# Six gate columns of a hybrid decoder layer as three Strassen pairs, behind an S5 branch with a shorter rhythm

## The chip, the cores and the metric

The kernel runs on one core of a Trainium2 chip. Its time is the device time of one launch in microseconds (us). An engine's name is short: PE is TensorE (matmul), DVE is VectorE, ACT is ScalarE, POOL is GpSimd, SP is the sync engine, which here issues nearly all DMA transfers.

## What is computed

One decoder layer on 1024 tokens of width 1024, in float32. All of the input projection's columns are products of the same normalised input `h`:

```python
h = rms_norm(x, g_pre[i])
proj = h @ w_in[i]
s5_x, s5_g, lru_x, lru_g, gate_s, gate_l = jnp.split(proj, IN_SPLITS, axis=-1)
y_s = s5_ssm(s5_x, ...)                  # zoh discretisation, complex diagonal scan, C s + D u
glu_a, glu_b = jnp.split(jax.nn.gelu(y_s) @ w_glu[i], 2, axis=-1)
y_s = glu_a * jax.nn.sigmoid(glu_b) * jax.nn.silu(s5_g)
z_s = y_s @ w_bs[i]
c = causal_depthwise_conv(lru_x, ...)
y_l = rg_lru(c, ...)
z_l = (y_l * jax.nn.silu(lru_g)) @ w_bl[i]
merged = jax.nn.sigmoid(gate_s) * z_s + jax.nn.sigmoid(gate_l) * z_l
x = x + rms_norm(merged @ w_out[i], g_post[i])
x = x + (p[i] @ w_ple[i]) * jax.nn.sigmoid(x @ w_ple_gate[i])
```

`w_in` has 44 column blocks of 128. Numbers in the kernel count these: 0 to 3 are the S5 input, 4 to 7 the S5 gate (two of them, 4 and 5, are made early), 28 to 35 `gate_s` and 36 to 43 `gate_l`.

## The kernel before

**Matmuls.** Activations lie transposed: 128 channels on the partitions, 1024 tokens along the row. To keep float32 accuracy with a faster matmul type, each operand is split into a rounded "hi" and the remainder "lo", and each product of a 128x128 weight block with 512 tokens is three matmuls, hi x hi, hi x lo and lo x hi (`three`; lines 317 and 319 issue them). One column block of `w_in` has 8 weight blocks and 2 halves of tokens, so 48 matmuls. The kernel calls a column whose product only passes a sigmoid (or SiLU) and is stored a *light* column: `light` makes it in a wide PSUM tile `ps_L` of two banks, ACT takes the sigmoid into `sg` (L1015), DVE multiplies for SiLU (L1017), and SP stores it (L1019) to `sgl_d`, `sgs_d` or `sil_d` in DRAM, from where a later stage reads it.

**Weights.** `Weights` walks a plan of *quads* (four 128x128 blocks), made in advance. Per quad: SP loads raw weights (L163, two quads at a time, four such buffers `wraw`), POOL makes sums where a Strassen product needs them (L194), ACT copies the hi part (L222) into one of six ring buffers `wq`, and DVE subtracts to get the lo part (L234). For `w_bs`, `w_out` and `w_ple_gate`, ACT writes minus hi instead (L225) and a DMA of POOL's queue adds the raw weights to it (L226). Weight loads are issued eight quads ahead, but each needs a raw buffer that its last reader has left. Later stages of the kernel already use Strassen's form, in which a 2x2 block product takes 7 products and some sums in place of 8.

**S5.** The S5 branch runs as a background generator (`bg`), one step per `tick()`, and a tick comes every 12 matmuls of the foreground columns. `s5_params` prepares on the 32 groups: exponentials, a sine and cosine (`cosp`, L613), the powers `pw` of the step (L618 to L632, twenty small POOL operations), the zoh factor (POOL L638 to L659, with one reciprocal on DVE, L644), `bb` (POOL L681 to L683). `powers_zoh` (DVE L669 to L675) writes `pzt`, `turn` transposes it on PE (`pwT`, L691) and stores it to `pt_d`. `s5_ladders` (DVE L847 to L856) builds rotation tables `etab`. The input `u` takes a detour through DRAM (`u_d`) to change its layout.

Then there are eight blocks. In a block (`s5_main`), DVE finishes `wn` (L913, L915; loaded from `pt_d`, L882), PE makes `pkt` (L928), ACT copies it to `kt` (L931) and SP stores it in eight pieces to a Toeplitz table `toep` (L934), PE makes `pin` (L939), ACT copies it to `pq` (L946), DVE turns it (L950 to L953), scans (L960) and turns it back (L964 to L972), and PE makes `py` (L983, L984), which ACT passes through GELU (L986) a step into the next block. POOL prepares the next block's output weights `ca` meanwhile (`s5_out_weights`, L902 to L904) and `dd` (L917).

**Order.** Each engine runs its own instructions in the order in which the program issues them; a step of the background that is issued in one tick stands at that point in the queues of all engines. The foreground while S5 runs is eighteen light columns, 36 to 43, then 28 to 35, then 4 and 5.

Of the kernel before, what the change touches and what calls it, by code (L numbers as in the profile page):

```python
# [9 lines left out]
F32 = mybir.dt.float32  # L10
# [23 lines left out]
F_ROWS = (0, 1, 4, 2, 5, 3, 6, 7)  # L34


def weight_plan():
    blocks, quads = [], []
# [24 lines left out]
    for m in (*range(36, 44), *range(28, 36), 4, 5):  # L63
        plain(col("w_in", m, range(ND)))

# [48 lines left out]
    return blocks, quads  # L114


BLOCKS, QUADS = weight_plan()
# [18 lines left out]
class Weights:  # L136
# [42 lines left out]
    def sum(self, upto):  # L179
        G = self.nc.gpsimd  # L180
        while len(self.ready) <= min(upto, len(QUADS) - 1):
# [3 lines left out]
            s = self.sums  # L185
            if q[0] == "O2" and len(self.done) < i:
# [20 lines left out]
            if q[0] in ("S4", "O4"):  # L207
                add("S4", "A12", "S2", ALU.subtract, "S2")
# [4 lines left out]
    def make(self, upto):  # L213
        nc = self.nc
        while len(self.done) <= min(upto, len(QUADS) - 1):
# [8 lines left out]
            if q[0] == "plain" and BLOCKS[q[1][0]][0] in self.BY_DMA and i < len(QUADS) - 2 * ND:  # L224
# [28 lines left out]
def tile_hybrid_trunk(  # L253
# [20 lines left out]
    page_pool = {i: pages for i in range(14)}  # L274
# [11 lines left out]
    pt_d = dram.tile([2, 8, 32 * P], F32, name="pt_d")  # L286

# [251 lines left out]
    def s5_params():  # L539
# [78 lines left out]
        G.tensor_tensor(pw_r[:, 1, :], mag, cosp[:, 0:32], ALU.mult)  # L618
        G.tensor_tensor(pw_i[:, 1, :], mag, sinp[:, 0:32], ALU.mult)
        for n in (1, 2, 4):  # L620
# [6 lines left out]
            G.tensor_tensor(t, ai, bi, ALU.mult)  # L627
            G.tensor_tensor(dr, ar, br, ALU.mult)
            G.tensor_tensor(dr, dr, t, ALU.subtract)
            G.tensor_tensor(t, ai, br, ALU.mult)  # L630
            G.tensor_tensor(di, ar, bi, ALU.mult)
            G.tensor_tensor(di, di, t, ALU.add)  # L632
# [63 lines left out]

    prep = s5_params()
    def prep_all(n):
        for i, _ in enumerate(prep):
            if i % n == n - 1:  # L700
                yield
# [132 lines left out]
    cosv = cosp[:, 32:].rearrange("p (m i) -> p m i", m=8)  # L834
    sinv = sinp[:, 32:].rearrange("p (m i) -> p m i", m=8)
    s5 = {}

    e_tab = {}

    def s5_ladders():  # L840
        t = page(6, "etab", F32)
        e1 = t[:, :512].rearrange("p (r i n) -> p r i n", r=2, i=16)
        e2 = t[:, 512:768].rearrange("p (r i n) -> p r i n", r=2, i=16)
        tm = t[:, 768:1024].rearrange("p (r i n) -> p r i n", r=2, i=16)
        e_tab[1], e_tab[2] = e1, e2
        for e, m0, steps in ((e1, 1, 4), (e2, 5, 3)):
            V.memset(e[:, 0, :, 0:1], 1.0)  # L847
            V.memset(e[:, 1, :, 0:1], 0.0)
            for m in range(steps):
                n = 1 << m  # L850
                er, ei = (v[:, m0 + m, :].unsqueeze(1).unsqueeze(3).to_broadcast([P, 2, 16, n]) for v in (cosv, sinv))
                src, dst, t_ = e[:, :, :, 0:n], e[:, :, :, n:2 * n], tm[:, :, :, :n]
                V.tensor_tensor(dst, src, er, ALU.mult)
                V.tensor_tensor(t_, src, ei, ALU.mult)
                V.tensor_tensor(dst[:, 0], dst[:, 0], t_[:, 1], ALU.subtract)
                V.tensor_tensor(dst[:, 1], dst[:, 1], t_[:, 0], ALU.add)  # L856
                if m % 2:
                    yield
# [47 lines left out]
    def s5_main(hb, table, before):  # L906
# [13 lines left out]
        yield  # L920
        before()
        s5_load(hb + 1)
        yield

# [773 lines left out]
```

## Time and profile before

| | |
|---|---|
| median of three timed runs | 928.27 us (928.26 to 928.28) |
| the profiled execution | 928.25 us |
| its span in the trace | 926.5 us |
| PE busy | 919.0 us, 99% |
| DVE busy | 624.6 us, 67% |
| ACT busy | 469.1 us, 51% |
| POOL busy | 150.6 us, 16% |

The span runs from the first to the last recorded instruction. Rows of a timeline give start and duration in us, the engine, the line, the operation and its operands; in brackets, where there is one, the idle time before it and what ended it. Matmuls are pipelined, so their durations overlap; what counts is the distance from one start to the next.

### The profile page before, as it was taken

To read this page: it belongs to the slowest core of one execution; us is meant where nothing else is said; L and a number is where in the kernel's file an instruction comes from. 1 tells how busy PE (TensorE), PEld (TensorE's weight loads), DVE (VectorE), ACT (ScalarE), POOL (GpSimd) and SP (SyncE) were. 2 spreads that over 40 slices of the span, in tenths; PEclk is the share of its full clock that TensorE was granted. 3 is DMA by queue.
4 is the path that set the end of the run, shared out by engine and by line. 5 is a ranking of instruction groups with operands and counts; after the bars stand their busy time and mean duration, and the time that the engine had idled before them with its cause. 6 is when DMAs were issued, how large, how long until landed. Compare 5 with 4: busy or idle time off the path is not lost.

```text
span 926.5 us, 11716 instructions
## 1 busy us (share of the span) xinstructions
PE 919.0 (99%) x4228; PEld 760.3 (82%) x4228; DVE 624.6 (67%) x977; ACT 469.1 (51%) x714; POOL 150.6 (16%) x159
## 2 busy tenths in 40 slices
PE   9999999999999999999999999999999999999997
PEld 7888888888888888888888888888888887887886
DVE  6885566666664347766666767687862798886863
ACT  6643233444443356666666668544534355558531
POOL 1218112212220000000000000022322126422100
PEclk9999999999999999999999999999999999999999
DMA  9745445564533201111111116811479975499951
GB/s 358 277 126 160 126 142 166 172 171 133 173 97 113 74 29 52 52 46 51 52 52 52 47 34 216 291 56 55 141 255 244 247 193 206 119 245 233 301 184 56
DMA packets 70442, 134.21 MB, mean 145 GB/s; under 512 B 18416, under 2 KB 32880, under 8 KB 70384
## 3 DMA queue, kind: packets, MB, share of 16 engines
q1 hardware_dynamic: 64768, 122.72, 41.7%
q0 software_dynamic: 5472, 10.49, 6.3%
q8 instruction: 33, 0.54, 0.2%
q10 hardware_dynamic: 144, 0.26, 0.1%
q14 instruction: 25, 0.20, 0.1%
HBM read 95.30 MB, written 27.53 MB: 133 GB/s over the span
## 4 chain that ended last, share of the span: by engine, by line
PE 89%; issue 6%; DMA 2%; DVE 1%; POOL 1%; ACT 0%; POOLq 0%; SPq 0%
PE ps_L L319 16%; PE ps_L L317 8%; PE ps_rx L319 8%; PE ps_rg L319 8%; PE ps_rg L317 4%; PE ps_rx L317 4%; PE ps_F L319 3%; PE ps_u L319 3%; PE bZ L319 3%; PE ps_pg L319 2%; PE bW L319 2%; PE pg L319 2%; PE bX L319 2%; PE ps_ple L319 2%; PE ps_ea L319 2%
## 5 line engine op out<-in xcount | busy, mean ns | idle before, releaser
L319 PE MATMUL ps_L<-hB,wq 128*128 128x512 f32 x640 | 197.4, 390 | 0.0
L319 PEld LDWEIGHTS ps_L<-hB,wq 128*128 128x128 f32 x640 | 120.3, 188 | 24.3
L317 PE MATMUL ps_L<-hB,wq 128*128 128x512 f32 x320 | 127.1, 397 | 0.0
L222 ACT ACTIVATE wq<-wraw 128x512 fp32r<-128x512 f32 (+1 forms) x188 | 112.5, 613 | 24.1 <-issue 9.2
L234 DVE TENSOR_TENSOR wq<-wraw,wq 128x512 fp32r<-128x512 f32 (+1 forms) x152 | 105.0, 706 | 3.1 <-ACT wq L222 3.1
L319 PE MATMUL ps_rg<-hB,wq 128*128 128x512 f32 x320 | 98.5, 389 | 0.0
L319 PE MATMUL ps_rx<-hB,wq 128*128 128x512 f32 x320 | 98.5, 389 | 0.0
L319 PE MATMUL ps_pg<-x1hl,wq 128*128 128x512 f32 x240 | 74.9, 392 | 0.3 <-DVE x1hl L1374 0.2
L317 PEld LDWEIGHTS ps_L<-hB,wq 128*128 128x128 f32 x320 | 60.2, 188 | 13.3 <-issue 1.7
L319 PEld LDWEIGHTS ps_rg<-hB,wq 128*128 128x128 f32 x320 | 60.1, 188 | 12.5
L319 PEld LDWEIGHTS ps_rx<-hB,wq 128*128 128x128 f32 x320 | 60.1, 188 | 12.4
L194 POOL TENSOR_TENSOR wS<-wraw 128x512 f32<-128x512 f32 x8 | 12.4, 1549 | 354.8 <-DMA wraw<-w_blocks 343.3
L1078 DVE SCALAR_TENSOR_TENSOR c<-ps_rx,cp_t,c 128x1023 f32<-128x1023 f32 (+2 forms) x30 | 38.5, 1282 | 46.2 <-ACT c L1076 45.5
L317 PE MATMUL ps_rx<-hB,wq 128*128 128x512 f32 x160 | 62.3, 389 | 0.0
L317 PE MATMUL ps_rg<-hB,wq 128*128 128x512 f32 x160 | 62.3, 389 | 0.0
L319 PEld LDWEIGHTS ps_pg<-x1hl,wq 128*128 128x128 f32 x240 | 44.8, 188 | 11.5 <-DVE x1hl L1374 1.7
L1015 ACT ACTIVATE sg<-ps_L 128x1024 f32<-128x1024 f32 x20 | 20.5, 1027 | 59.7 <-issue 52.5
L226 POOL DMA_DIRECT2D wq<-wraw x36 | 31.8, 883 | 100.1 <-ACT wq L225 65.6
L317 PE MATMUL ps_pg<-x1hl,wq 128*128 128x512 f32 x120 | 47.0, 391 | 0.0
L319 PE MATMUL ps_u<-hB,wq 128*128 128x512 f32 x128 | 39.8, 392 | 0.4 <-DVE hB L736 0.4
L319 PE MATMUL ps_F<-ys,wq 128*128 128x512 f32 x128 | 39.4, 389 | 0.0
L1086 ACT ACT_TABLE_LOAD x9 | 11.5, 1283 | 51.2 <-DVE yr L1115 51.2
(360 smaller groups left out, 1927.0 us busy)
## 6 DMA issues: line engine op xcount, KB each, us to landing
wraw<-w_blocks SPq DMA_DIRECT2D x95, 512.0 KB
wq<-wraw POOLq DMA_DIRECT2D x36, 256.0 KB, 6.0
xt<-x_t SPq DMA_DIRECT2D x8, 512.0 KB
ple_d<-ple_sb SPq DMA_DIRECT2D x8, 512.0 KB
wn<-sbt SPq DMA_DIRECT2D x8, 512.0 KB
sgl_d<-sg SPq DMA_DIRECT2D x8, 512.0 KB
wn<-pt_d SPq DMA_DIRECT2D x16, 256.0 KB
sgs_d<-sg SPq DMA_DIRECT2D x8, 512.0 KB
```

The costliest lines, as they stand in the source:

```text
L194: G.tensor_tensor(s[name], s[a], s[b], op)
L222: nc.scalar.activation(hi, src, AF.Copy)
L226: nc.gpsimd.dma_start(lo.bitcast(F32), src, accum_op=ALU.add)
L234: self.nc.vector.tensor_tensor(lo, src, hi.bitcast(F32), ALU.subtract)
L317: T.matmul(ps, wh, xh, start=start, stop=False, skip_group_check=more)
L319: T.matmul(ps, a, b, start=False, stop=stop and a is (wh if xl_last else wl), skip_group_check=more)
L1015: S.activation(t, ps, AF.Sigmoid)
L1078: V.scalar_tensor_tensor(c[:, d:], ps[:, :NT - d], w_[3 - d], c[:, d:], ALU.mult, ALU.add)
L1086: S.activation(sq, ps, AF.Sigmoid)
```

## The change

1. **The six gate columns 30 to 35** become three pairs (30 and 31, 32 and 33, 34 and 35). Each pair is a Strassen product over the two halves of the 1024 inputs, the two columns and the two halves of the tokens: seven products of four weight blocks x 3 matmuls. They run after S5 has ended, with their sums of weights on DVE instead of POOL, the lows of their unsummed weights through the accumulating DMA, and their sums of `h` (`T1` to `T4`) built from copies of `h` that go to DRAM (`h_d`) in the prologue, eight stores of 512 KB on SP, and come back in four loads of 1 MB. Results are stored by halves (`gate_out`). The wide PSUM tiles are closed for the pairs and opened again after them.
2. **S5 takes five steps per block instead of seven**: `pkt` and `pin` come in one step, and the step behind `before()` goes. Beside S5 stand twelve light columns, 4 and 5 first, then 36 to 43, 28 and 29. S5 is put on the background list before the last of the `u` columns starts, and its first block comes 84 matmuls after `u` has ended instead of 180.
3. `py` takes a wide PSUM tile instead of a `px` bank.
4. The twenty operations of the powers move from POOL to DVE, and the ladders become a background task of their own that starts with the sine.
5. The scratch memory for DMA descriptors is set to 8192 bytes, and a page 19 is added.

```diff
+PAIRS = (30, 32, 34)
...
-    for m in (*range(36, 44), *range(28, 36), 4, 5):
+    for m in (4, 5, *range(36, 44), *range(28, PAIRS[0])):
         plain(col("w_in", m, range(ND)))
+    first = [b for ks in (lo, hi) for m in PAIRS for b in col("w_in", m, ks)]
+    for o in range(0, len(first), 8):
+        light.add(chunk(first[o:o + 8]))
+        cut((len(blocks) - len(first[o:o + 8]), len(first[o:o + 8])))
+    for m in PAIRS:
+        c0, c1 = (chunk(col("w_in", m + i, range(ND))) for i in range(2))
+        light.add(c0)
+        quads.extend((part, c0, c1, 4) for part in ("O2", "S1", "S3", "S4", "A22"))
...
-                G.tensor_tensor(s[name], s[a], s[b], op)
+                (self.nc.vector if light else G).tensor_tensor(s[name], s[a], s[b], op)
...
-            if q[0] == "plain" and BLOCKS[q[1][0]][0] in self.BY_DMA and i < len(QUADS) - 2 * ND:
+            if q[0] in ("plain", "A22") and (q[1] in LIGHT or BLOCKS[q[1][0]][0] in self.BY_DMA
+                                             and i < len(QUADS) - 2 * ND):
                 nc.scalar.activation(lo, src, AF.Copy, scale=-1.0)
                 nc.gpsimd.dma_start(lo.bitcast(F32), src, accum_op=ALU.add)
...
-        G.tensor_tensor(pw_r[:, 1, :], mag, cosp[:, 0:32], ALU.mult)
-        G.tensor_tensor(pw_i[:, 1, :], mag, sinp[:, 0:32], ALU.mult)
+        V.tensor_tensor(pw_r[:, 1, :], mag, cosp[:, 0:32], ALU.mult)
+        V.tensor_tensor(pw_i[:, 1, :], mag, sinp[:, 0:32], ALU.mult)
...
+        nc.sync.dma_start(h_d[k], xt(k))
...
         before()
         s5_load(hb + 1)
-        yield
-
+        if hb == 7:
+            h_load(2, "T2", "B22")
...
+        pin = px.tile([P, 2, 2, P], F32, tag="px", name=f"pin{hb}")
+        for g in range(4):
+            T.matmul(pin[:, g // 2, g % 2, :], win[:, g, :], U[:, g, :], start=True, stop=True)
         for g in range(4):
             S.activation(kt[:, g, :], ps[32 * g:32 * g + 16, :P], AF.Copy)
...
-            ps = px.tile([P, HT], F32, tag="px", name=f"py{hb}")
+            ps = wide(f"py{hb}")[:, :HT]
...
-        for _ in prep:
-            yield
-        for _ in range(3):
-            yield
-        yield from s5_ladders()
+        for at in prep:
+            if at == "trig":
+                bg.append(s5_ladders())
+            yield
         turned[0]()
-        yield
-        yield
+        for _ in range(4):
+            yield
         turn()
         yield
         s5_load(0)
+        h_load(7, "T1", "B12")
         yield from s5_table(0)
+        h_load(8, "T3", "B11")
         s5_out_weights(0)
...
+    lu = quarter(page(15, "lu", F32))
+    xs = [px.tile([P, HT], F32, tag="px", name=f"lX{p_}") if p_ < 2 else gbank(0, "lX2") for p_ in range(3)]
+    for p_ in range(3):
+        if p_ != 1:
+            tick()
+        lprod(xs[p_], hq["B11"], True)
+        S.activation(lu[:, p_], xs[p_], AF.Copy)
+        tick()
+    for p_, m in enumerate(PAIRS):
+        o = gp.tile([P, NT], F32, tag="c", name=f"lo{p_}", bufs=2)[:, HALF[0]]
+        lprod(xs[p_], hq["B21"], False)
+        gate_out(m, 0, o, xs[p_])
+        tick()
+    for p_, m in enumerate(PAIRS):
...
+        lprod(z, lop["T2"], True)
+        V.tensor_tensor(z, z, u, ALU.add)
+        S.activation(u, z, AF.Copy)
+        tick()
+        lprod(w_, lop["T1"], True)
+        S.activation(gb, w_, AF.Copy)
+        V.tensor_tensor(w_, w_, u, ALU.add)
+        tick()
+        lprod(z, lop["T3"], False)
+        V.tensor_tensor(gb, gb, z, ALU.add)
+        gate_out(m + 1, 1, gb, gb)
+        tick()
+        lprod(w_, hq["B22"], False)
+        gate_out(m, 1, u, w_)
+        lprod(z, lop["T4"], False)
+        gate_out(m + 1, 0, o, z)
...
-    nc = bacc.Bacc("TRN2", target_bir_lowering=False, num_devices=1)
+    nc = bacc.Bacc("TRN2", target_bir_lowering=False, num_devices=1, dynamic_dma_scratch_size=8192)
```

The order of instructions shows three places.

SP at the front of S5, where the transposed powers are stored and read back. Before:

```order
L163 DMA wraw_989<-w_blocks 128x1024
L1019 DMA sgl_d<-sg_982 128x1024
L694 DMA pt_d<-pzt 128x4x128
L163 DMA wraw_1070<-w_blocks 128x1024
L882 DMA wn_1022<-pt_d 128x1x512 x2
L882 DMA wn_1108<-pt_d 128x1x512 x2
```

Now:

```order
L830 DMA u_d<-up_887 1024x1x64 x2
L1091 DMA fT_932<-h_d 128x4x512
L706 DMA pt_d<-pzt 128x4x128
L1091 DMA fT_988<-h_d 128x4x512
L172 DMA wraw_873<-w_blocks 128x1024
L897 DMA wn_926<-pt_d 128x1x512 x2
L897 DMA wn_1017<-pt_d 128x1x512
```

One weight load still stands between the store to `pt_d` and the loads of `wn`, and two loads of `h` stand around the store. The weight load takes the raw buffer whose last reader is the low of `wq_820`. On DVE that low stands behind the ladders, which now come after `pzt`:

```order
L686 TENSOR_TENSOR pzt<-pzt 128x256
L687 TENSOR_TENSOR pzt<-pzt,sgn 128x256
L720 MEMSET etab 128x16
...
L728 TENSOR_TENSOR etab<-etab 128x16x4
L729 TENSOR_TENSOR etab<-etab 128x16x4
L245 TENSOR_TENSOR wq_820<-wraw_553,wq_820 128x512
```

Before, the ladders stood ahead of `pzt`, and POOL made the powers; now DVE runs the powers, the reciprocal, `pzt`, the ladders and then this low.

ACT in a block of S5, from one GELU to the next block's `pq`. Before:

```order
L986 ACT_TABLE_LOAD
L986 ACTIVATE ysb_1286<-py_1287 128x512
L931 ACTIVATE kt_1319<-pkt_1320 16x128 x4
L222 ACTIVATE wq_1338<-wraw_989 128x512
L946 ACTIVATE pq_1374<-pin_1353 64x256 x4
L1015 ACT_TABLE_LOAD
L1015 ACTIVATE sg_1389<-ps_L_1268 128x1024
```

Now, block 1:

```order
L1002 ACT_TABLE_LOAD
L1002 ACTIVATE ysb_1160<-py_1161 128x512
L950 ACTIVATE kt_1181<-pkt_1182 16x128 x4
L1034 ACT_TABLE_LOAD
L1034 ACTIVATE sg_1209<-ps_L_1082 128x1024
L232 ACTIVATE wq_1213<-wraw_873 128x512
L962 ACTIVATE pq_1230<-pin_1187 64x256 x4
```

`kt` and `pq` now come from PE's same step, and in this block a table load, a sigmoid and a weight copy stand between them; in most other blocks `pq` follows `kt` directly.

ACT and SP where the pairs begin. ACT now:

```order
L1034 ACTIVATE sg_2321<-ps_L_2223 128x1024
L232 ACTIVATE wq_2347<-wraw_1952 128x512
L236 ACTIVATE wq_2347<-wraw_1952 128x512
L1145 ACTIVATE lu<-lX_2339 128x512
L1063 ACTIVATE lT_2364<-fT_988 128x512 x4
L1116 ACTIVATE lT_2370<-fT_2168 128x512 x4
L232 ACTIVATE wq_2375<-wraw_1952 128x512
L236 ACTIVATE wq_2375<-wraw_1952 128x512
L1145 ACTIVATE lu<-lX_2340 128x512
```

and SP now:

```order
L1038 DMA sgs_d<-sg_2220 128x1024
L172 DMA wraw_2379<-w_blocks 128x1024
L1038 DMA sgs_d<-sg_2321 128x1024
L1130 DMA sgs_d<-lo_2425 128x512
```

The weight copies `wq_2347` and `wq_2375` belong to the pairs' first products; between them stand the copy of the first product to `lu` and eight copies of the sums of `h`. The load of `wraw_2379` stands ahead of the store of the last light column.

More of the change, by code (lines that the diff above doesn't have):

```diff
@@ L34 @@
 F_ROWS = (0, 1, 4, 2, 5, 3, 6, 7)
+PAIRS = (30, 32, 34)
 def weight_plan():
-    blocks, quads = [], []
+    blocks, quads, light = [], [], set()
     def chunk(names):
@@ L113, in weight_plan @@
             cut(c)
-    return blocks, quads
-BLOCKS, QUADS = weight_plan()
+    return blocks, quads, light
+BLOCKS, QUADS, LIGHT = weight_plan()
 FIRST = ("O2",)
@@ L207, in sum @@
             if q[0] in ("S4", "O4"):
-                add("S4", "A12", "S2", ALU.subtract, "S2")
+                add("S4", "A12", "S2", ALU.subtract, "A12" if light else "S2")
             if q[0] == "S3":
@@ L934, in s5_main @@
             nc.sync.dma_start(toep[j::8, :, 16 * j:P], kt[:, :, 0:P - 16 * j])
-        yield
-        pin = px.tile([P, 2, 2, P], F32, tag="px", name=f"pin{hb}")
-        for g in range(4):
-            T.matmul(pin[:, g // 2, g % 2, :], win[:, g, :], U[:, g, :], start=True, stop=True)
+        if hb == 7:
+            h_load(6, "T4", "B21")
         next(table, None)
@@ new lines, in tile_hybrid_trunk, with t_build, lprod @@
+    page_pool.update({i: gp for i in (14, 15, 16, 17)})
+    def t_build():
+        lpage("T1", 1)
+        t_low("T1")
+        yield
+        t_high("T3")
+        lpage("T3", 1)
+        lpage("T4", 0)
+        for k in range(4):
+            S.activation(lop["T4"][0][:, k, :], lf["T4"][:, k], AF.Copy)
+        yield
+        t_low("T3")
+        yield
+        lpage("T4", 1)
+        t_low("T4")
+    def lprod(ps, op, start):
+        W.ahead()
+        for k, wb in enumerate(W.next()):
+            three(ps, wb, (op[0][:, k, :], op[1][:, k, :]), start and k == 0, k == 3, not start)
```

129 lines of the change are left out of this document (94 added, 35 removed).

## The prediction

> **What bounds the kernel now.** I read the page first, then PE's waits, then PE's timeline around the S5 branch, and last the rows of the engines that feed it.
>
> ```profile
> span 926.5 us, 11716 instructions
> PE 919.0 (99%) x4228; PEld 760.3 (82%) x4228; DVE 624.6 (67%) x977; ACT 469.1 (51%) x714; POOL 150.6 (16%) x159
> PE warm L500 <- DVE halfpi L291: 1.1, 1, 1.1
> ...
> 300.00:320.00 20.00, 20.00 (x90) 16.57 (x89) 8.50 (x10) 6.53 (x9) 0.00 (x0) 1.00 0.20 65
> 840.00:860.00 20.00, 20.00 (x97) 16.57 (x96) 12.79 (x27) 17.39 (x31) 7.62 (x9) 1.00 0.95 213
> ```
>
> TensorE is busy for 919.0 of 926.5 us and its longest wait (line, what it waited for, total, times, longest) is the 1.1 us at the very start. The two rows by stretch (20 us, then busy time of PE, its weight loads, DVE, ACT, POOL, and last the granted clock, the DMA engines' share and GB/s) show PE full at a granted clock of 1.00. So every matmul taken out is worth its issue time, and every wait that the change makes on PE is paid in full: no idle time stands there to absorb it. The profiled execution took 928.25 us, 0.02 under the median of 928.27; 1.75 us of it lie outside the span. The sum below is on 928.25.
>
> The issue time, and the rhythm of S5, stand in PE's timeline (start, duration, engine, line, operation):
>
> ```profile
> 78.00 0.39 PE L317 MATMUL ps_L<-hB,wq 128*128 128x512 f32 x1
> 102.49 0.60 PE L691 MATMUL pwT<-ident,pzt 128*128 128x128 f32 x4
> 122.56 0.61 PE L939 MATMUL pin<-U,wn 128*128 128x128 f32 x4
> 189.53 1.05 PE L939 MATMUL pin<-U,wn 128*128 128x128 f32 x8
> 191.79 0.39 PE L317 MATMUL ps_L<-hB,wq 128*128 128x512 f32 x1
> 193.83 0.39 PE L317 MATMUL ps_L<-hB,wq 128*128 128x512 f32 x1
> ```
>
> Nine matmuls from 191.79 to 193.83 are 0.2267 us each (the durations overlap). Between the pins at 122.56 and 189.53 lie three blocks: 22.32 us each, of which 84 matmuls are 19.04 and S5's own PE work 3.28.
>
> **What is removed.** Three pairs of columns cost 3 x 96 = 288 matmuls; as Strassen pairs they are 3 x 7 products of 12, 252. 36 fewer at 0.2267 is **-8.16 us**. That is all the gain: PE has nothing else to win.
>
> **Term 1, the front of S5.** pwT now stands 24 matmuls after 78.00, at 83.44, instead of 102.49. What must be ready by then is pzt.
>
> ```profile
> 71.93 0.24 DVE L613 TENSOR_SCALAR cosp<-scratch 128x160 f32<-128x160 f32 x1
> 72.25 0.25 POOL L618 TENSOR_TENSOR pw<-scratch,cosp 128x32 f32<-128x32 f32 x1 [20.90 <-DVE cosp L613]
> 79.49 0.25 POOL L638 TENSOR_TENSOR scratch<-scratch 128x32 f32<-128x32 f32 x1
> 80.83 0.35 DVE L644 RECIPROCAL scratch<-scratch 128x32 f32<-128x32 f32 x1 [8.66 <-POOL scratch L642]
> 84.38 1.09 POOL L681 TENSOR_TENSOR bb<-braw,scratch 128x512 f32<-128x512 f32 x1
> 92.30 1.49 POOL L904 TENSOR_TENSOR ca<-ca,t 128x576 f32<-128x576 f32 x1
> 92.53 1.40 DVE L855 TENSOR_TENSOR etab<-etab 128x128 f32<-128x128 f32 x1
> 93.86 1.55 DVE L856 TENSOR_TENSOR etab<-etab 128x128 f32<-128x128 f32 x1
> 98.10 0.22 DVE L856 TENSOR_TENSOR etab<-etab 128x64 f32<-128x64 f32 x1
> 98.24 0.42 DVE L669 TENSOR_TENSOR pzt<-pw,scratch 128x256 f32<-128x256 f32 x1
> 100.61 0.43 DVE L675 TENSOR_TENSOR pzt<-pzt,sgn 128x256 f32<-128x256 f32 x1
> ```
>
> cosp is ready at 72.17 as before. The 20 power operations took POOL 7.3 us (72.25 to L638 at 79.5); on DVE I take 4.05, 0.2 each from the small etab rows. With the reciprocal and POOL's zoh chain after it (3.7 before beside DVE's lows, 2.4 by its own rows), zoh is ready at about 79.1 instead of 84.4. Then pzt's seven operations, 2.8 us alone (98.24 to 101.04). But now they stand beside POOL's bb, cc and ca operations, eight large ones from 84.38 in the old order, and the rows show what that does: L855 and L856 on DVE take 1.40 and 1.55 us beside POOL's 1.49 and end just after a POOL operation ends, where the half-sized one alone takes 0.22. Two-input operations of the two engines take turns. Each of pzt's seven then costs about 1.1 in place of 0.4: ready at some 86.9, PE late by 3.5.
>
> Behind it DVE runs the ladders (6 us alone) and the low of wq_820, with two or three POOL operations left to take turns with: done at about 96.8. SP has a load, wraw_873, that waits for that low, and the loads wn<-pt_d queue behind it.
>
> ```profile
> 103.75 0.38 SPq L694 DMA_DIRECT2D pt_d<-pzt  x1
> 108.75 2.50 SPq L882 DMA_DIRECT2D wn<-pt_d  x4
> 114.05 1.23 DVE L913 TENSOR_TENSOR wn<-wn 128x1024 f32<-128x1024 f32 x1 [9.07 <-DMA wn<-pt_d]
> 115.31 0.69 DVE L915 TENSOR_TENSOR wn<-wn 128x512 f32<-128x512 f32 x1
> ```
>
> From the issue of wn's loads to DVE's first use are 5.3 us, the two operations 1.9: 96.8 + 0.35 + 5.3 + 1.9 = 104.4. PE would reach the first pin at 98.0 (60 matmuls and pwT after 83.44). So the front costs **+6.5** in all, the 3.5 at pwT included. If the turn-taking costs DVE half, both waits shrink to +3; if the two h_d loads of 1 MB, which SP issues around pt_d's store, hold up wn, +9.
>
> The eight stores of h_d (4.2 MB) go out on SP between 32 and 50 us, ahead of one weight load. I cost them at nothing:
>
> ```profile
> 66.51 0.24 DVE L607 TENSOR_SCALAR scratch<-scratch 128x160 f32<-128x160 f32 x1
> 69.35 1.28 ACT L608 ACT_TABLE_LOAD   x1
> ```
>
> DVE's part before the sine ends at 66.75, and ACT's table load for the sine at 70.63, so 3.9 us cover a late low ahead of it. Without that cover the stores would shift S5's parameters by 1 to 5 us.
>
> **Term 2, the blocks.** A block now has 60 matmuls beside it: 13.60 + 3.28 = 16.88 us between pins on PE, not 22.32.
>
> ```profile
> 192.28 0.69 DVE L950 TENSOR_TENSOR ta<-pq,tt 128x512 f32<-128x512 f32 x1 [2.75 <-ACT pq L946]
> 194.96 3.64 DVE L960 TENSOR_TENSOR_SCAN q<-r,q 128x128 f32<-128x128 f32 x4
> 194.73 1.40 POOL L903 TENSOR_TENSOR t<-pw,cc 128x576 f32<-128x576 f32 x1 [9.77 <-DMA toep<-kt]
> 204.79 0.69 DVE L915 TENSOR_TENSOR wn<-wn 128x512 f32<-128x512 f32 x1
> 206.05 1.28 ACT L986 ACT_TABLE_LOAD   x1 [5.66 <-issue]
> 209.17 1.11 ACT L931 ACTIVATE kt<-pkt 16x128 f32<-16x128 f32 x4 [0.71 <-issue]
> 213.37 1.03 ACT L1015 ACTIVATE sg<-ps_L 128x1024 f32<-128x1024 f32 x1
> ```
>
> The next pin needs the next wn. From the pin at 189.53 it is 2.75 us to ta, and 13.2 more to wn's end at 205.48: 15.95. That fitted into 22.32 with 6 to spare; into 16.88 it fits by 0.9. The change puts kt's four copies (1.11) between the pin and pq on ACT, since pkt and pin come in one step; there is about one low less in the chain (0.6). So an ordinary block ends even. In block 1 and block 5 ACT also does a table load, a sigmoid and a weight's high part (1.28 + 1.03 + 0.62 = 2.9) ahead of pq: 2.8 where ACT has no lead, 1.4 where half of it is done before the pin. A third block has one low more, 0.5. Sum **+4.8**. Below: +1, if ACT does these before the pin; above: +8, if the chain lengthens by 0.5 in every block.
>
> The dots of py go to a wide PSUM tile: the last half of ps_L is evicted before it is wanted, so nothing waits; without that cover it would be one sigmoid, 1.03, per block, inside the upper end.
>
> **Term 3, the first products of the pairs.** The light lows come from an accumulating DMA of POOL's queue, and the next weight's load on SP waits for it; behind that load stands the store sgs_d<-sg_2321, and the first copy to lu on ACT waits for that store, since its page lies in the region that S5 frees.
>
> ```profile
> L226 POOL DMA_DIRECT2D wq<-wraw x36: 850/859/1209, 698.5 to 867.5; - x36
> DMA to landing us min/median/max: 3.2/6.0/11.1
> 697.05 0.62 ACT L222 ACTIVATE wq<-wraw 128x512 fp32r<-128x512 f32 x1
> 697.58 0.62 ACT L225 ACTIVATE wq<-wraw 128x512 fp32r<-128x512 f32 x1
> ```
>
> Counted from the last pin: the lo copy of wq_2274 ends on ACT at +18.2 (it stands behind the eight copies of T1 and T2). The DMA lands 3.2 to 11.1 us after issue, in stretches whose DMA share was up to 0.95; here the engines are quiet (0.20 at 300:320), so I take 3.5, near the fast end: +21.8. Load and store are issued by +22.6. For the store no landing is shown; 3.3, from the same fast end, gives +25.9. Then lu's copy, eight T copies and the two copies of wq_2375, eleven that start 0.53 us apart as the two rows at 697 do: 6.0, +31.9, and its DMA again 3.5: +35.4. PE asks for it 132 large matmuls, one py and one pin later, at +32.4. **+3.0**; at 6.0 per DMA it is +7.6, at 3.2 throughout +2.
>
> [...]
>
> The rest of the pairs runs without a wait by the same chains: 12 matmuls (2.7 us) a product against at most two lows or sums of 0.69 on DVE. That the later columns' weights start from another ring position costs nothing, since loads are issued eight quads ahead.
>
> **Sum:** -8.16 + 6.5 + 4.8 + 3.0 = +6.1, so 928.25 + 6.1 = 934.4; I say **934**.
>
> **The rivals.** *The S5 chain keeps up* (faster). If DVE and POOL overlap better than the old rows show, ACT runs its sigmoid ahead of the pin, and the DMAs land in 3.2, the lower ends add to 3 + 1 + 2 = 6, and 928.25 - 8.2 + 6 = 926.1; with the front covered too, 923. It decides from waits of under 6.3 us in all. For it: POOL is idle between 72 and 79 in the new order and might finish part of bb's work early. Against it: bb needs zoh, the same value that pzt needs. *Gain and waits cancel:* waits of 6.3 to 10, within 1.9 us of before. For it: the three terms hang on one chain, and a wait at pwT gives ACT and SP time for later ones. *The DMA queues fill up* (worse): the stores of h_d delay the weight loads and the prologue by the 5 us named, and the h_d loads delay wn by 3 more: 942. For it: the stretch from 40 to 60 us had a DMA share of
>
> ```profile
> 40.00:60.00 20.00, 20.00 (x90) 16.57 (x89) 19.49 (x61) 10.85 (x17) 7.56 (x7) 1.00 0.60 181
> ```
>
> 0.60, which 4.2 MB more would fill; against it: PE needs no more weights there than before. That the change doesn't remove the 36 matmuls is excluded: PE's order has 3780 rows before and 3744 after.
>
> **How the numbers follow.** The forecast, waits of 10 to 20 us, has 0.46, the keeping-up case 0.31, cancelling 0.14, and full queues 0.09. The measurement can tell 0.2%, 1.9 us, from no change: faster is below 926.4, slower above 930.1. The chances: faster 0.31, same 0.14, slower 0.55. The likeliest case's own range is 930 to 940. To hold the time 8 times in 10 the range reaches into the keeping-up case to 922 and, at the upper end, to the start of the full queues, 941.
>
> **What would show it.** In the new profile PE waits for pwT on DVE's pzt and for the first pin on wn (term 1); in the blocks for wn before the third and the seventh pin, and the chain of DVE's operations is nearly without gaps (term 2); in the pairs for wq_2375 with its releaser a DMA, and ACT stands before lu on the store (term 3). Each DVE operation beside POOL's bb work takes over 1 us. If PE's waits between 78 and 330 us sum to under 6, I am wrong about the whole; if they sum to 14 but stand elsewhere, about the mechanism.

## The result: 1.6% slower

The changed kernel takes **942.77 us** (median of four runs, 942.38 to 943.78) against 928.27: a ratio of **1.0157**, interval [1.014, 1.0175]. The forecast was 934, with 922 to 941 around it. The direction was right, the size was not, and the time lies outside the range. One of the twelve runs of x6 below took 1538.97 us at a mean granted clock of 0.556 and is left out of x6's figures.

The profiled run took 942.38 us. The head of its page, and the waits of PE between 78 and 330 us (line, what it waited for, total, times, longest; "issue" means that the profile names no releaser):

```profile
span 940.6 us, 11829 instructions
PE 915.2 (97%) x4192; PEld 757.1 (80%) x4192; DVE 664.9 (71%) x1050; ACT 493.1 (52%) x763; POOL 150.3 (16%) x148
```

```profile
PE pin L948 <- issue: 6.4, 1, 6.4
PE lX L329 <- ACT lu L1145: 4.3, 2, 2.7
PE pin L948 <- DVE wn L930: 3.2, 4, 1.9
PE pin L948 <- ACT ysb L1002: 1.6, 1, 1.6
PE pwT L703 <- DVE etab L721: 1.1, 1, 1.1
PE py L1000 <- DVE q L988: 0.7, 2, 0.5
```

The waits sum to 17.3 us, where the forecast had 14.3. PE is now busy 915.2 of 940.6 us. PE has 36 rows fewer, 4192 for 4228, but its busy time fell by 3.8 and not by 8.16: some of its work ran slower. Where that was is in the table by stretch (the length, busy time of PE, weight loads, DVE, ACT and POOL, then the granted clock, the DMA share and GB/s):

```profile
102.00:104.00 2.00, 0.00 (x0) 0.00 (x0) 0.23 (x1) 0.00 (x0) 0.00 (x0) 0.58 0.91 315
104.00:106.00 2.00, 0.18 (x1) 0.21 (x2) 1.97 (x3) 0.00 (x0) 0.00 (x0) 0.50 1.05 375
106.00:108.00 2.00, 2.00 (x9) 2.00 (x10) 1.12 (x4) 0.10 (x1) 0.00 (x0) 0.50 0.95 243
108.00:110.00 2.00, 2.00 (x8) 1.55 (x7) 0.52 (x1) 1.42 (x4) 0.00 (x0) 0.71 0.55 159
216.00:218.00 2.00, 2.00 (x7) 1.70 (x7) 1.60 (x4) 1.30 (x4) 0.00 (x0) 0.50 0.89 248
```

TensorE's granted clock falls to 0.50 while PE stands before the first pin and stays there for about three microseconds after it has work again (0.50 to 108, 0.71 from 108 to 110); a second such place follows the seventh pin (0.50 from 216 to 218). Before, it was 1.00 in all these stretches, for example:

```profile
104.00:106.00 2.00, 2.00 (x11) 1.64 (x10) 0.98 (x3) 0.24 (x1) 0.00 (x0) 1.00 0.99 393
```

The span grew by 14.1, and 8.16 of work is gone, so 22.3 us were lost. I assign them by the distances between PE's pins (at 105.82, 124.76, 143.30, 160.12, 177.51, 194.73, 214.73 and 233.13) and by the waits:

| part | forecast | measured |
|---|---|---|
| front: first pin at 105.82, not 98.0 | 6.5 | 7.8 |
| blocks: seven periods sum to 127.31, not 118.16; the clock's part taken off | 4.8 | 5.8 |
| pairs: two waits on `lu` | 3.0 | 4.3 |
| clock, at the first and the seventh pin | none | 3.4 |
| behind the pairs, to the end (PE waits there 1.1 on a weight's DMA) | none | 0.3 |

That is 21.6; some 0.7 is not assigned. The clock's 3.4 is an estimate: the missing share of the granted clock times PE's busy time, over these stretches, about 1.7 at each pin.

**Front.** The timeline of DVE, POOL, PE and SP's queue:

```profile
77.54 0.46 DVE L681 TENSOR_TENSOR pzt<-pw,scratch 128x256 f32<-128x256 f32 x1 [0.43 <-POOL scratch L661]
79.30 1.32 POOL L693 TENSOR_TENSOR bb<-braw,scratch 128x512 f32<-128x512 f32 x1
79.61 1.29 DVE L684 TENSOR_TENSOR pzt<-pw,scratch 128x256 f32<-128x256 f32 x1
82.13 1.40 DVE L686 TENSOR_TENSOR pzt<-pzt 128x256 f32<-128x256 f32 x1
84.76 0.44 PE L703 MATMUL pwT<-ident,pzt 128*128 128x128 f32 x2 [1.06 <-DVE etab L721]
...
96.61 1.85 SPq L897 DMA_DIRECT2D wn<-pt_d  x3
103.77 1.22 DVE L928 TENSOR_TENSOR wn<-wn 128x1024 f32<-128x1024 f32 x1 [3.28 <-DMA wn<-pt_d]
105.03 0.69 DVE L930 TENSOR_TENSOR wn<-wn 128x512 f32<-128x512 f32 x1
105.82 2.05 PE L948 MATMUL pin<-U,wn 128*128 128x128 f32 x8 [6.45 <-issue]
```

The releaser `etab L721` of `pwT` is a small operation right behind `pzt`'s last one, which ends at 84.70; the first pin starts 0.1 after `wn`'s last operation. The loads of `wn` go out when forecast (96.61 against 96.8 + 0.35), but DVE gets them 7.2 us after, not 5.3.

**Blocks.** ACT's delay and the taking of turns meet ahead of the third pin (143.30). DVE's first operation on the result of the pin before, its last one on the next `wn`, and POOL's operation beside that:

```profile
129.87 0.69 DVE L966 TENSOR_TENSOR ta<-pq,tt 128x512 f32<-128x512 f32 x1 [2.75 <-ACT pq L962]
141.39 1.22 POOL L917 TENSOR_TENSOR ca<-pw,cc 128x576 f32<-128x576 f32 x1 [2.19 <-PE py L1000]
141.44 1.71 DVE L930 TENSOR_TENSOR wn<-wn 128x512 f32<-128x512 f32 x1
```

`ta` starts 5.1 us after the pin at 124.76, not 2.75, and `wn` is ready at 143.15 (its last operation takes 1.71 beside POOL's, and 0.69 at 105.03 with nothing of POOL's beside it). The page puts this pin's wait down to `ysb`, which ends at 143.27; but the next pin starts at 160.12, ahead of its own block's `ysb` (161.21), so I take `wn` as the releaser.

**Pairs.** ACT's and SP's rows from the last GELU to the second copy to `lu`:

```profile
253.14 2.56 SPq L1004 DMA_DIRECT2D y_d<-ysb  x4
255.81 0.39 SPq L172 DMA_DIRECT2D wraw<-w_blocks  x1
256.30 0.38 SPq L1038 DMA_DIRECT2D sgs_d<-sg  x1
261.64 0.60 ACT L1145 ACTIVATE lu<-lX 128x512 f32<-128x512 f32 x1 [5.16 <-DMA sgs_d<-sg]
262.14 2.18 ACT L1063 ACTIVATE lT<-fT 128x512 fp32r<-128x512 f32 x4
264.22 2.18 ACT L1116 ACTIVATE lT<-fT 128x512 fp32r<-128x512 f32 x4
267.34 0.58 ACT L1145 ACTIVATE lu<-lX 128x512 f32<-128x512 f32 x1
267.97 0.50 PE L329 MATMUL lX<-hB,wq 128*128 128x512 f32 x1 [2.67 <-ACT lu L1145]
```

The chain into `lu` is the forecast one, with the store taking 5.3 us from issue to the copy where 3.3 was forecast. PE stops at the `lu` copies themselves, not at `wq_2375`.

### The profile page after: what moved, and what is told of

Same layout as the page of the kernel before. It is cut to its first block, busy times and chain, and to the rows that moved or that the text cites. A ratio compares the mean times of both kernels' runs of the same rounds, so it can differ in the third digit from the quotient of the medians.

```text
span 940.6 us, 11829 instructions
## 1 busy us (share of the span) xinstructions
PE 915.2 (97%) x4192; PEld 757.1 (80%) x4192; DVE 664.9 (71%) x1050; ACT 493.1 (52%) x763; POOL 150.3 (16%) x148
## 4 chain that ended last, share of the span: by engine, by line
PE 74%; DVE 8%; DMA 7%; issue 5%; ACT 4%; POOL 1%; SPq 0%; ACTq 0%; POOLq 0%; DVEq 0%
PE ps_rg L331 8%; PE ps_rx L331 8%; PE ps_pg L331 6%; PE ps_L L331 5%; PE ps_rx L329 4%; PE ps_rg L329 4%; PE ps_pg L329 3%; PE bZ L331 3%; PE ps_L L329 3%; PE ps_u L331 2%; DMA wn<-pt_d 2%; PE bX L331 2%; PE pg L331 2%; PE bW L331 2%; PE lZ L331 2%
## 5 line engine op out<-in xcount | busy, mean ns | idle before, releaser
L331 PE MATMUL ps_L<-hB,wq 128*128 128x512 f32 x448 | 139.3, 392 | 0.0
L232 ACT ACTIVATE wq<-wraw 128x512 fp32r<-128x512 f32 (+1 forms) x191 | 114.5, 613 | 30.0 <-DMA wraw<-w_blocks 10.3
L245 DVE TENSOR_TENSOR wq<-wraw,wq 128x512 fp32r<-128x512 f32 (+1 forms) x146 | 101.3, 709 | 14.7 <-ACT wq L232 14.7
L331 PEld LDWEIGHTS ps_L<-hB,wq 128*128 128x128 f32 x448 | 85.1, 190 | 17.9 <-DVE wq L245 0.3
L329 PE MATMUL ps_L<-hB,wq 128*128 128x512 f32 x224 | 89.0, 398 | 0.0
L331 PEld LDWEIGHTS ps_rg<-hB,wq 128*128 128x128 f32 x320 | 60.1, 188 | 12.5
L237 POOL DMA_DIRECT2D wq<-wraw x45 | 39.6, 879 | 167.0 <-ACT wq L236 136.3
L329 PEld LDWEIGHTS ps_L<-hB,wq 128*128 128x128 f32 x224 | 42.7, 190 | 8.5
L329 PEld LDWEIGHTS ps_rg<-hB,wq 128*128 128x128 f32 x160 | 30.0, 188 | 6.2
```

The source lines that it names most:

```text
L232: nc.scalar.activation(hi, src, AF.Copy)
L237: nc.gpsimd.dma_start(lo.bitcast(F32), src, accum_op=ALU.add)
L245: self.nc.vector.tensor_tensor(lo, src, hi.bitcast(F32), ALU.subtract)
L329: T.matmul(ps, wh, xh, start=start, stop=False, skip_group_check=more)
L331: T.matmul(ps, a, b, start=False, stop=stop and a is (wh if xl_last else wl), skip_group_check=more)
```

## The experiments

Twelve kernels ran. Each is the changed kernel with the edit shown; times are medians, ratios are to the kernel before on the same chip.

**x1: the first block's `wn` out of the queue.** Its loads go on ACT's queue and its two operations ahead of half the table.

```diff
-            nc.sync.dma_start(t[:, 0, r],
+            (nc.sync if hb else nc.scalar).dma_start(t[:, 0, r],
...
+        s5_wn(0)        # the two wn operations of block 0, taken out of s5_main
+        yield from tab  # second half of s5_table(0)
```

> The changed kernel, with block 0's loads of wn from pt_d on ACT's queue instead of SP's, and DVE's two wn operations ahead of half of its table work. Queue theory (the loads stood behind a weight load that waits for the low of wq_820, and PE's 6.45 us before the first pin came from that): that wait falls under 1 us, the granted clock stays 1.00 between 100 and 120 us, and the time falls by 6.45 + 1.75 = 8.2, to about 934.6. Rival (wn is late because the DMA engines are full with the loads of h, or a later pin takes the wait up): the first pin moves by under 2 us, time 941 or more.

Measured **934.80**, ratio 1.0068 [1.0053, 1.0083]. The first pin is at 99.11 without a wait:

```profile
88.84 1.25 ACTq L897 DMA_DIRECT2D wn<-pt_d  x2
97.06 1.22 DVE L923 TENSOR_TENSOR wn<-wn 128x1024 f32<-128x1024 f32 x1
99.11 1.13 PE L953 MATMUL pin<-U,wn 128*128 128x128 f32 x8
PE pin L953 <- DVE kt L956: 2.6, 1, 2.6
```

The granted clock is 1.00 from 100 to 120. The front's wait and its clock drop together were worth 8.0, net of what came back at once: the second pin now waits 2.6 (last row; 0.5 in the changed kernel), since about 3 us of DVE's work that stood ahead of the two `wn` operations (half of the table, a SiLU multiply of 1.2) now stands behind them, from 98.92 on. The edit moves the loads and DVE's operations together, so it doesn't say how much each is worth.

**x2: is the clock a cost of its own?** 24 more matmuls stand in the wait before the first pin; they write the bank that `pin` then overwrites, so the kernel only does more.

```diff
+        if hb == 0:
+            for _ in range(24):
+                T.matmul(pin_flat, hx[:, :P], hx, start=True, stop=True)
```

> The changed kernel with 24 extra matmuls (5.4 us, their result is overwritten) on PE between the first pkt and the first pin, inside the 6.45 us in which PE waits there; nothing else differs. Clock theory (the idle time itself halves the granted clock for the first microseconds after it): the first pin starts where it did, 105.8, the clock stays 1.00, and the time falls by 1.75 us to 941.0 although more work is done. Rival (the lower clock has another cause, or the slower records are no real time): 942.8, or more if the extra matmuls get in the way.

Measured **940.21**, ratio 1.0126 [1.0111, 1.0141]: 2.6 us faster with more work, and the clock is whole:

```profile
104.00:106.00 2.00, 0.93 (x5) 0.43 (x3) 1.90 (x3) 0.00 (x0) 0.00 (x0) 1.00 1.05 373
106.00:108.00 2.00, 1.93 (x12) 1.75 (x13) 1.41 (x5) 0.72 (x2) 0.00 (x0) 1.00 0.93 234
```

The first pin moved by only 0.25 (106.07), and the stretch from it to the eighth shrank by 1.76. The lower clock is a loss apart from the wait ahead of it. The profiled runs differ by 2.2; 1.5 of it lies up to the eighth pin, and the other 0.7 behind the pairs, where the edit changes nothing, so the clock's own part is nearer 1.8 than 2.6.

**x3: the first `lu` in another page.** `lu` takes a page that is free early, and one page of `T1` the one in the freed S5 region, with its hi copies moved behind the first products.

```diff
-    lop = {"T2": [3, 19], "T1": [9, 16], "T3": [17, 2], "T4": [7, 8]}
+    lop = {"T2": [3, 19], "T1": [15, 16], "T3": [17, 2], "T4": [7, 8]}
-    lu = quarter(page(15, "lu", F32))
+    lu = quarter(page(9, "lu", F32))
```

> The changed kernel with lu on a page outside the region that S5 frees (it takes page 9, and the hi part of T1 goes to page 15), and with the hi copies of T1, T3 and T4 on ACT behind the three copies to lu. Theory (PE's 4.3 us in the pairs are waits for lu, the first for the store of the last light column, the second for the copies queued ahead on ACT): both waits vanish, time 938.5. Rival (the accumulating DMA of wq_2375 or the late T copies take their place): PE waits there for wq or lT instead, time 941 or more.

Measured **939.35**, ratio 1.0117 [1.0102, 1.0132]. The waits at `lX` are gone, and one of 1.2 at `lZ` on `lu` is new. From the last pin to the first matmul behind the pairs it is 77.84 us instead of 81.22, so 3.4 were won. (The four runs lie between 937.69 and 940.78, and the profiled one is the slowest: its eight blocks are 2.8 longer than the changed kernel's.) So the waits hang on `lu`'s page and on the copies ahead of it on ACT; the edit moves both and doesn't separate them.

**x4: `pq` a step earlier**, right behind `kt`, ahead of the sigmoid and the weight copies of blocks 1 and 5.

```diff
-        yield
-
         pq = wk.tile([P, 4, P], F32, tag="pq", name=f"pq{hb}")...
             ... S.activation(pq[...], pin[...], AF.Copy)
+        yield
```

> The changed kernel with pq's four copies issued in pin's own step, so that on ACT they come ahead of the table load, the sigmoid and the weight copy in blocks 1 and 5. Theory (these three put 2.8 us into DVE's chain, hence the waits before the third pin, 1.65, and around the seventh, 2.6 with py's, and the half-rate clock after that, 1.6): these waits go, time about 937. Rival (DVE with POOL beside it needs the whole 16.9 us of a block, whatever ACT does): the waits spread over other pins, time 941 or more.

Measured **939.67**, ratio 1.0123 [1.0106, 1.014]. The waits before the third and the seventh pin are gone, as forecast for ACT's part; 1.65 and 1.62 appear before the sixth and the eighth. Ahead of the sixth, DVE's L930 again takes 1.66 beside POOL's L917 (at 192.83 and 192.72). So ACT was one part of the reason, worth 3.1, and x5 tries the other.

**x5: POOL's work beside other DVE work.** The scratch of `s5_out_weights` shares a buffer with `kt`, so POOL's L918 waits in each block until `toep` has left `kt`, about 10 us. Here it takes part of a ladder's table that is no longer read.

```diff
-        t9 = wk.tile([P, 576], F32, tag="kt", ...)
+        t9 = (e_tab[0][:, 1024:1600] if hb > 1 else wk.tile([P, 576], F32, tag="kt", ...))
```

> The changed kernel with POOL's scratch of the output weights of blocks 2 to 7 in a free part of the ladders' page instead of in kt's buffer, so that L918 and L919 no longer wait until kt has been stored and run right behind py, where DVE waits for pq, instead of beside DVE's second half of the block. Theory (the old collision costs DVE some 3 us a block, which is what makes its chain longer than the 16.9 us between pins): DVE's L987 to L930 take 0.4 to 0.7 again, PE's waits from the third pin on (1.65, 0.45, 0.32, 2.6) and the half-rate clock after the seventh (1.64) go, time about 936. Rival (the waits come from ACT's table load and sigmoid ahead of pq in blocks 1 and 5 alone): they stay there, time 941 or more.

Measured **936.43**, ratio 1.0088 [1.0075, 1.0101]. The groups of DVE's operations (busy time, mean ns of one) in the changed kernel and then in x5:

```profile
L988 DVE TENSOR_TENSOR q<-ta,tb 64x254 f32<-64x254 f32 x16 | 9.7, 607 | 0.2
L930 DVE TENSOR_TENSOR wn<-wn 128x512 f32<-128x512 f32 x8 | 8.5, 1067 | 0.3
L886 DVE TENSOR_TENSOR tt<-tt,sb 128x256 f32<-128x256 f32 x8 | 6.5, 810 | 0.2
```

```profile
L988 DVE TENSOR_TENSOR q<-ta,tb 64x254 f32<-64x254 f32 x16 | 6.7, 419 | 0.2
L930 DVE TENSOR_TENSOR wn<-wn 128x512 f32<-128x512 f32 x8 | 5.5, 692 | 0.3
L886 DVE TENSOR_TENSOR tt<-tt,sb 128x256 f32<-128x256 f32 x8 | 3.4, 426 | 0.2
PE pin L948 <- DVE wn L930: 1.8, 3, 0.9
```

The same operations are 0.2 to 0.4 us shorter each, the pins' waits behind the first fall to 1.8 in all, and three periods in a row are 16.86 or 16.87; the drop at the seventh pin is gone. This single line is worth 6.3 us, more than the 4.8 I gave the whole term. The kernel before has the same collisions on its own q operations (in its groups L972 has a mean of 631 ns) but not on `wn` and `tt` (692 and 426 ns), and had 6 us of slack for them.

**x6: x1, x3, x4 and x5 together.**

> The four edits together: wn of block 0 through ACT's queue and early on DVE, lu's page, pq in pin's step, POOL's scratch. Theory (the waits are separate and add): left are 0.9 at pwT, some 2 at the second pin, 1.2 in the pairs and 0.4 late, so 928.3 - 8.2 + 4.9 = about 925, faster than the kernel before. Rival (a common limit, DVE's share of work in the S5 stretch, turns up elsewhere): 930 or more.

Measured **928.11** (eleven runs, 926.57 to 934.96), ratio 1.0013 [0.9996, 1.003]: no difference, where 925 was expected. In the profiled run, which is the slowest of the eleven, PE now stands 5.1 at the pairs' second kind of product, and the clock is at 0.68 from 265 to 275:

```profile
244.83 3.68 SPq L1009 DMA_DIRECT2D y_d<-ysb  x4
248.62 0.93 SPq L1047 DMA_DIRECT2D sgs_d<-sg  x1
255.08 2.19 ACT L1072 ACTIVATE lT<-fT 128x512 fp32r<-128x512 f32 x4 [4.63 <-DMA sgs_d<-sg]
269.32 0.80 PE L329 MATMUL lZ<-lT,wq 128*128 128x512 f32 x1 [5.13 <-ACT lu L1171]
```

The move of x3 only changed who uses the freed region first: now `T1`'s copies wait for the same store, which stands behind the `y_d` stores on SP, and the lows and sums of the pairs bunch up behind it on DVE. How much of this the faster runs have, no profile shows. It pointed to the queue rather than the page, which x9 tries.

**x7: the S5 rhythm without the pairs.** Columns 30 to 35 are light columns again and nothing of `h` is copied; it computes the same.

```diff
-    for m in (4, 5, *range(36, 44), *range(28, PAIRS[0])):
+    for m in (4, 5, *range(36, 44), *range(28, 36)):
...
-        nc.sync.dma_start(h_d[k], xt(k))
-        h_load(7, "T1", "B12")
-        h_load(8, "T3", "B11")
```

> The changed kernel without the pairs: columns 30 to 35 are plain light columns again, behind 29, and the stores and loads of h are left out; S5 keeps its five steps and its place. Theory (the pairs save 36 matmuls, 8.16, and cost the 4.3 us for lu and 0.4 late; the rest of the loss belongs to S5): 942.8 + 8.2 - 4.7 = 946.3. Rival (the traffic of h makes wn land late, 7.2 us instead of 5.3 after its issue, and with the clock behind it): the first pin comes 1.9 or more earlier, time about 943.

Measured **944.63**, ratio 1.0174 [1.0159, 1.0189]. The pairs, taken by themselves, bring 1.9 us of their 8.16; without them the first pin comes at 104.86, so the copies of `h` cost the front 1.0. DVE still gets `wn` only 6.5 us after the issue of its loads (96.33 to 102.81), so of the 1.9 above the forecast 5.3 the copies of `h` explain 0.7; the rest is open. This kernel is 16.4 slower than the one before: of the 22.3 lost, about 16 belong to S5's shorter rhythm and earlier start and about 6 to the pairs.

**x8: the powers back on POOL.**

```diff
-        V.tensor_tensor(pw_r[:, 1, :], mag, cosp[:, 0:32], ALU.mult)
+        G.tensor_tensor(pw_r[:, 1, :], mag, cosp[:, 0:32], ALU.mult)
   (and the eighteen operations behind it)
```

> The changed kernel with the twenty operations of the powers on POOL, as before. Theory (POOL's 0.25 to 0.46 an operation in place of DVE's 0.2 to 0.3, and zoh behind them): zoh is ready some 3 to 4 us later, pzt too, PE waits some 4.5 instead of 1.06 at pwT, and the first pin comes about 3 later, time about 946. Rival (DVE is the fuller engine there, and the ladders that bound the first pin gain from the 4 us that it saves): the first pin comes no later, time 942.8 or less.

Measured **948.27** (946.16, 946.38, 950.17 and 950.23), ratio 1.0214 [1.0198, 1.023]. In the profiled run (950.23) PE stands 4.53 and 0.53 before `pwT`, the clock is at 0.57 behind that (90 to 92), and the first pin comes at 110.0. This part of the change is worth 3.4 to 7.5 us: DVE was the right place.

**x9: the queues at the hand-over.** The last block's `y_d` stores go on POOL's queue, the store of column 29 on ACT's, and the hi copies of `T4` come a tick later.

```diff
-                nc.sync.dma_start(y_d[b][:, g0 + g], ysb[:, g])
+                (nc.sync if hb < 7 else nc.gpsimd).dma_start(y_d[b][:, g0 + g], ysb[:, g])
-            nc.sync.dma_start(dst, t)
+            (nc.scalar if wm == 29 else nc.sync).dma_start(dst, t)
...
         lpage("T3", 1)
+        yield
         lpage("T4", 0)
```

> The changed kernel with three transfers of the hand-over from S5 to the pairs moved: the y stores of the last block go out on POOL's queue, the last light store (column 29) on ACT's queue, and the second load that feeds the lu copies is read by PE one tick later. Theory (the 4.3 us of waits on the lu copies come from the gate store standing behind the y stores on SP and from the second copy standing behind eight T copies on ACT): the two waits of 1.67 and 2.67 fall to under 1 together, 942.8 - 3.5 to 4.3 = about 939. Rival (the load waits for every last user of the freed S5 pool, wherever those are queued, and the store's landing of 5.2 is what sets it): the first wait stays over 1.2, and the time is 941 to 942.

Measured **939.75**, ratio 1.013 [1.0117, 1.0144]:

```profile
255.29 0.34 ACTq L1038 DMA_DIRECT2D sgs_d<-sg  x1
260.88 0.60 ACT L1146 ACTIVATE lu<-lX 128x512 f32<-128x512 f32 x1 [4.06 <-DMA sgs_d<-sg]
PE lX L329 <- ACT lu L1146: 1.2, 2, 0.6
```

The two waits fall from 4.3 to 1.2. The store leaves ACT as soon as its sigmoid is done; its 5.6 us from issue to copy stay, so what was saved is the queue and the eight copies.

**x10 and x11: the parts together.** x11 is x1, x4, x5 and x9; x10 adds that the two SiLU columns stand behind columns 36 to 39, so that their multiplies of 1.2 us leave the front of S5.

```diff
-    for m in (4, 5, *range(36, 44), *range(28, PAIRS[0])):
+    for m in (*range(36, 40), 4, 5, *range(40, 44), *range(28, PAIRS[0])):
```

> The edits of x1, x4, x5 and x9 together, without the lu page of x3. Theory (the losses are the front, the clock, the block waits and the pairs' lu copies, and each of these edits takes its own): what is left over 928.3 - 8.2 = 920.1 is the wait at pwT (1.1), the wait at the second pin with its clock drop (2.6 and 1.4), the eighth pin (0.9) and some 0.5 in the blocks: about 926. Rival (in the pairs a new wait takes the place of each one removed, as in x6): 928 to 930.

> x11 with the SiLU columns 4 and 5 placed after columns 36 to 39, so that their multiplies of 1.2 us each on VectorE leave the front, where the second block's factors are made. Theory: the 2.6 at the second pin and the clock drop behind it go, 926 - 3 = about 923, faster than both kernels. Rival (the second pin's wait is set by POOL's part of the factors and not by VectorE's queue): the wait stays over 2 and the time is within 1 of x11.

x11: **927.10**, ratio 0.9984 [0.9975, 0.9992]. x10: **922.62** (921.87 to 923.14), ratio **0.994** [0.9926, 0.9953], faster than both kernels. All that PE still waits for between 78 and 330 us, first in x11, then in x10:

```profile
PE pin L953 <- DVE wn L924: 3.6, 2, 2.6
PE pwT L703 <- DVE etab L721: 0.9, 1, 0.9
```

```profile
PE pwT L703 <- DVE etab L721: 1.1, 1, 1.1
PE pin L953 <- DVE wn L924: 0.9, 1, 0.9
```

With the multiplies out of the front, the second pin's wait of 2.6 is gone, and six of the seven periods are 16.83 to 16.87, the 16.88 of the prediction. x10 and x11 differ by 4.5, of which the pins' distances explain 2.7; the profiled runs, 920.8 and 923.4 in span, differ by 2.6. x11's median is 1.9 above its profiled run, and that goes with the clock: its two runs with a mean granted clock of 1.000 took 924.86 and 925.22, the nine with 0.998 or 0.999 took 926.43 to 927.56. Where the clock fell in those nine no profile shows; x6's profile shows slower matmuls behind the same wait of 2.6: three of them take 1.40 from 120.38 to 121.78, where three take 0.68 from 125.22 on.

**x12: x10 without the pairs.**

> x10 without the pairs: columns 30 to 35 are light columns again, the copies of h and the sums of h are gone, everything else of x10 stays (column 29's store is an ordinary one in the middle now). It computes the same. Theory (in x10 S5 runs without loss and the pairs pay their 36 matmuls in full): 922.6 + 8.2 = 930.8, a little slower than before, since the waits at pwT (1.1) and the eighth pin (0.9) stay. Rival (the pairs still lose something that no wait on PE shows, or their traffic costs S5 something): 926 to 929.

Measured **929.54**, ratio 1.0011 [1.0002, 1.002]. The first matmul behind S5's stage is at 301.34, and before it was at 300.55; PE's one wait there is 0.8 at `pwT`. So the five-step rhythm, nearly without a wait, wins nothing and loses about 1.3 us: it only makes room. `py`'s wide tile and the descriptor memory of 8192 bytes are in x12 too, so the 1.3 holds their cost as well. The pairs are worth 6.9, between theory and rival; of the 1.3 missing from 8.16, 0.9 is x10's wait at the eighth pin, which x12 does not have.

## Why the prediction was wrong

**What bounds the kernel: right, with one clause wrong.** PE was full, each matmul was worth its issue time (x12 to x10: 6.9, and 0.9 for the eighth pin's wait, against 8.16), and each wait was paid. "Every wait that the change makes on PE is paid in full" failed: a wait of 6.4 was paid with more than its length, since the clock fell to 0.50 behind it. The sum put this at nothing, without a reason; it was 3.4 in the profiled run, and x2 took one of the two drops away by keeping PE at work through the wait. Of the 8.0 us between the sum, 934.4, and the profiled run, this is the largest part; the three terms were each 1.0 to 1.3 too small as well (table above), and 1.0 lies elsewhere. Without the clock's 3.4 the time would have been some 939.4, inside the range. At the first pin the clock fell in a wait of 6.45 (0.58 from 102 to 104, 0.50 from 104 to 108, 0.71 from 108 to 110); at the seventh pin it fell after shorter waits (last section). My own sum had the front's 6.5 in two waits, 3.5 at `pwT` and 3.0 at the first pin, and asked of neither what the clock does behind it.

**Term 1, the front: right in place, off in both pieces.** At `pwT` the wait was 1.06, not 3.5. That these operations of DVE and POOL take turns was right (1.29, 1.28 and 1.40 in the rows of `pzt`, 1.14 the last), but I let all seven collide; POOL's `bb` began only at 79.30, when three of the seven were done or under way at 0.43 to 0.46. The rows show a turn: DVE's operation that starts at 79.61 ends 0.28 after POOL's (80.90 and 80.62) and takes 1.29, where in the kernel before the same operation, with nothing of POOL's beside it, takes 0.42. The landing of `wn` took 7.2, not 5.3, with a DMA share of 0.76 and 0.91 in the last two stretches before it (100 to 104). x7 gives the copies of `h` 1.0 of the first pin's lateness, a third of the three that the rival of full queues named, and 0.7 of the landing's 1.9; the cause of the rest is open. The `h_d` stores themselves cost nothing, as I had it: the DMA share from 40 to 60 rose to 0.93, and `cosp` is ready at 72.1 as before.

**Term 2, the blocks: right in the first place, the cause half seen.** A block whose pin does not wait takes 16.82 to 16.87 (here, in x5 and in x10), the 16.88 of the sum. I gave the rest to ACT's table load and sigmoid in two blocks, and the waits do stand before the third and the seventh pin. x4 removed that part, won 3.1 and found 1.65 in other blocks; x5 took POOL's operations away from `wn` and `tt` and won 6.3. The collisions are in each period from the second on, also in the one of 16.82 (143.30 to 160.12), where the two `wn` operations take 2.25 and 1.79; there ACT has nothing ahead of `pq`, and the pin doesn't wait. I had the row for it: the old L903 on POOL waits 9.77 for `toep<-kt`, and in a shorter block that lands on DVE's last operations ahead of the pin. I used taking turns in the front and forgot it in the blocks.

**Term 3, the pairs: right chain, wrong last link.** Store to page to `lu` to the copies was right. The store took 5.3 from issue to the copy, not 3.3, which I had taken from the fast end of another transfer's landings. So PE stopped at the first and the second copy to `lu` (1.67 and 2.67), ahead of `wq_2375`, the weight that I had named. x9, with the queues mended, takes 3.1 of the 4.3 away. Two small sums of the prediction don't come out, neither of which moves the forecast: term 2's pieces 2.8, 1.4 and 0.5 make 4.7, not 4.8, and two DMAs at 6.0 instead of 3.5 make this term 8.0, not 7.6.

**The rivals.** "The S5 chain keeps up" is what x10 does: 922.62 against its 923 to 926, but only with five edits. "The DMA queues fill up" came nearest in time, 942, by a mechanism that holds 1.0 of it. Where I tied the three terms to one chain, so that early waits would give time to later ones, x1 shows it true in part (2.6 came back at the second pin), and it may be why single edits won less or more than their waits.

## What to carry to other kernels

When a background chain gets a shorter period, list every operation of it that meets another engine's, and ask what each meets at the new distance; slack had hidden collisions that a count of durations doesn't show. Here a wait of 6.4 us on a full TensorE cost its length and about 1.7 more at a granted clock of 0.50 (an estimate from the clock's share over 104 to 110), and work put into it, even useless, took that part away (x2); so here a forecast wait needed a term for the clock. At the hand-over between two memory regions here the last user of the old one set the start: look in which queue its store stands, before moving the pages about (x9 won 3.0, and x3's move of the page brought a new wait in x6).

## What was not expected of the hardware

The same waits do not always drop the clock. In the changed kernel and in x9 PE stands 0.5, 0.2 and 1.9 us within 5 us before the seventh pin. In the first the clock is 0.50 behind it (row above); in x9 it isn't:

```profile
216.00:218.00 2.00, 1.87 (x12) 1.75 (x13) 1.67 (x5) 1.45 (x5) 0.00 (x0) 1.00 0.18 31
110.00:112.00 2.00, 2.00 (x6) 1.55 (x5) 1.64 (x4) 0.00 (x0) 0.00 (x0) 0.50 0.10 19
```

At the first pin x9 is worse off, with 0.50 until 112 where the changed kernel had it until about 109 (0.71 from 108 to 110). What makes the difference, one profile of each kernel can't show. Waits of 1.7 and 2.7 at `lX` left the clock at 1.00 in the changed kernel (256 to 274); one of 2.65 brought it to 0.57 in x1 (260 to 262) and one of 2.5 to 0.50 in x4 (264 to 266). That runs of one kernel differ in this is plain from their mean granted clocks: x3's four took 937.69 us at 0.996, 939.02 and 939.67 at 0.994, and 940.78 at 0.990; x8's took 946.2 and 946.4 at 0.992 and 950.2 twice at 0.989.
